# Expert weights of a mixture-of-experts layer in packets of 8 KB instead of 4 KB

## The chip, the core and the metric

The kernel runs on one core of a Trainium2 chip. A core has a matrix engine (PE, with its weight loads shown as PEld), a vector engine (DVE), an activation engine (ACT), GpSimd (POOL) and a queue engine (SP) that here issues nearly all loads from HBM. The transfers themselves are done by 16 DMA engines that work beside the compute engines. The metric is device time in microseconds of one launch; the median of three runs of the kernel before is 1217.87 us (1216.93 to 1220.4).

## What is computed

One layer of a hybrid backbone on 512 tokens of 1024 channels, with 256 context tokens, in fp32. Three token mixers (retention, window attention, neighbourhood attention) are merged by gates and an output projection. Then comes the part that the change is about, an expert-choice SwiGLU mixture of 16 experts, where each expert takes its 64 best tokens:

```python
def expert_choice_ffn(h, w_router, w_gate, w_up, w_down):
    b, n, d = h.shape
    cap = CAPACITY_FACTOR * n // N_EXPERTS                    # 2 * 512 // 16 = 64
    aff = jax.nn.softmax((h @ w_router).astype(jnp.float32), axis=-1)
    gate, idx = lax.top_k(jnp.swapaxes(aff, 1, 2), cap)
    bidx = jnp.arange(b)[:, None, None]
    xe = h[bidx, idx]
    hid = jax.nn.silu(jnp.einsum('becd,edf->becf', xe, w_gate)) * jnp.einsum('becd,edf->becf', xe, w_up)
    ye = jnp.einsum('becf,efd->becd', hid, w_down) * gate[..., None].astype(h.dtype)
    return jnp.zeros_like(h).at[bidx, idx].add(ye)
...
        hx = modulate(rms_norm(x, g_ffn[layer]), mod_x[:, 3], mod_x[:, 4])
        x = x + mod_x[:, 5, None] * expert_choice_ffn(hx, w_router[layer], w_exp_gate[layer],
                                                      w_exp_up[layer], w_exp_down[layer])
    return rms_norm(x, g_final)
```

Each of `w_gate`, `w_up` and `w_down` is 16 matrices of 1024 x 1024 fp32 (4 MB each), 201 MB in all. The rest of the inputs is about 80 MB.

## The kernel before

**Up to the experts.** Until about 640 us the kernel projects, runs the three mixers and merges them. A "pump" (class `Pump`) feeds the projections of `w_in` and of the three output matrices to PE in between: each unit's raw weights are loaded into a buffer of tag `rw` (three of 4 KB a partition), split by ACT (line 294) and DVE (line 295) into a high and a low part in two buffers of tag `ws` (seven of 4 KB), and multiplied three times. The splits run two units ahead of PE, the loads three or more. Beside that, `mod_sums` adds up parts of `w_mod` on DVE (line 1160) from loads of 512 KB (line 1144), one step for every eight steps of the pump. Then the output projection, the router's logits, the selection of tokens and the experts follow.

**The experts' weights** come in 384 chunks of 512 KB, a chunk being 128 neighbouring rows of 1024 floats, one row of 4 KB to a partition. Their order is written out in `chunks` (line 1089 on): for each expert eight chunks of gate and eight of up, alternately, where the first two of each of the next expert stand ahead of this one's eight chunks of the down matrix. `fetch` (line 1103) takes a free buffer off the list `free` and issues the next chunk's load on SP (line 1116); `use` (line 1121) hands the oldest chunk to PE and puts its buffer back on the list. There are 36 buffers: nine of the pool `ring2` from the end of the mixers, four left by `mod_sums`, and 23 that the stages before the experts leave one after the other, of tags `u4` (19 buffers of 4 KB, which hold the normalised input, the mixers' outputs, the merged rows and the residual `acc` earlier), `ws` and `rw`. All loads stand in SP's queue in one order: a load that waits for its buffer holds up those behind it.

**An expert on PE.** `gate_up(e, k)` (line 1513) multiplies the 128 channels of chunk k with the gate and the up matrix, eight matmuls of 512 columns in the records. `hid` is turned by transposes (line 1562), then eight chunks of the down matrix follow (line 1576), and for every second expert the outputs are scattered onto `acc`. For expert 0 the token rows are picked by PE itself (`select`, line 1530) between the steps of `gate_up`; for the others `gather` (line 1453) fetches them by an indirect DMA of POOL. At the end `last_scatter` and `put` finish the last experts, normalise and store.

Of the kernel before, what the change touches and what calls it, by code (L numbers as in the profile page):

```python
# [49 lines left out]
def kernel(ctx, tc, x, c, cctx_x, c_ctx, w_mod, b_mod, g_mix, g_ffn, w_in, decay, ret_gn, w_ret,  # L50
# [8 lines left out]
    RW = 3  # L59
# [15 lines left out]
    U4p = ctx.enter_context(tc.tile_pool(name="u4p", bufs=19))  # L75
# [7 lines left out]
    psp = ctx.enter_context(tc.tile_pool(name="psp", bufs=1, space=bass.MemoryType.PSUM))  # L83

# [117 lines left out]
    hx_ = [[u4([P, 2, S], F32R, name=f"hx{i}{p}") for i in range(4)] for p in "hl"]  # L202
    hc_ = [[u4([P, 4, CTX], F32R, name=f"hc{i}{p}") for i in range(2)] for p in "hl"]

    def HX(k, lo=0):
        return hx_[lo][k // 2][:, k % 2, :]

    def HC(k, lo=0):
        return hc_[lo][k // 4][:, k % 4, :]
# [6 lines left out]
    def row_stat(i0, i1):  # L216
        for i in range(i0, i1):
            junk = ws([P, D], name="junk")
            A.activation(f32(junk), xs[i], AF.Square, accum_out=ssq[:, i:i + 1])
        rsqrt(rstd[:, i0:i1], ssq[:, i0:i1], 1.0 / D, i1 - i0)  # L220
# [60 lines left out]
    class InUnit:  # L281
# [43 lines left out]
    class ProjUnit:  # L325
# [95 lines left out]
    def pair(name):  # L421
        return [u4([P, 2, S], name=name) for _ in range(2)]

    def at(y, k):
        return y[k // 2][:, k % 2, :]

    ropes = {}

    def rope_table(i):
        ropes[i] = u4([P, 2, S], name="rope")  # L430
        SY.dma_start(ropes[i], rope[:, 2 * i:2 * i + 2, :])

    def rope_t(o, i, q):
        cos, sin = ropes[i][:, 0, :], ropes[i][:, 1, :]
# [172 lines left out]
    def proj_unit(br, d, w):  # L607
# [3 lines left out]
        def done(o):  # L611
# [5 lines left out]
            if br == 2:  # L617
                if d % 2 == 0:
                    for p in range(2):
                        mg[p].append(u4([P, 2, S], F32R, name="mg"))  # L620
                hi, lo = mg[0][-1][:, d % 2, :], mg[1][-1][:, d % 2, :]
                A.activation(hi, m_, AF.Copy, scale=0.5)
                V.scalar_tensor_tensor(lo, m_, 0.5, f32(hi), op0=OP.mult, op1=OP.subtract)
# [303 lines left out]
    def window(g):  # L927
# [31 lines left out]
        def value(b, ti):  # L959
# [8 lines left out]
            if ti == len(tiles) - 1:  # L968
                evac(yb[g][:, :, b * P:(b + 1) * P], PVs.pop(b)[:, :256].rearrange("p (i q) -> p i q", i=2))
# [119 lines left out]
    def gate_chunks(e, k0, k1):  # L1089
        for i in range(k0, k1):  # L1090
            for w in (w_g, w_u):
                chunks.append((w, e * D * FH + i * P * FH))

    gate_chunks(0, 0, KT)
    for e in range(NE):
        if e + 1 < NE:
            gate_chunks(e + 1, 0, AHEAD)
        for i in range(KT):
            chunks.append((w_d, e * D * FH + i * P * D))
        if e + 1 < NE:  # L1100
            gate_chunks(e + 1, AHEAD, KT)

    def fetch(most=99):
        while free and len(loaded) < len(chunks) and most:
            most -= 1
            tg = free.pop(0)
            if tg in ("rg", "mw", "mac"):
                t = ring2.tile([P, FH], F32, name="rg", tag=tg, bufs=dict(rg=9, mw=3, mac=2)[tg])
            elif tg == "u":
                t = u4([P, FH], name="rg")  # L1110
            elif tg == "z":
                t = rw([P, FH], "rg")
            else:
                t = wtile([P, FH], "rg")
            w, off = chunks[len(loaded)]
            ld = SY.dma_start(t, dap(w, off, [[FH, P], [1, FH]]))
            if len(loaded) >= PF:
                tc.keep_in_program_order(ld)
# [17 lines left out]
    def mod_sums():  # L1136
        steps = [(w, k) for w in (2, 3, 4, 5) for k in range(KT)]
        tiles = []

        def load():  # L1140
# [6 lines left out]
        load()  # L1147
        load()
        for i, (w, k) in enumerate(steps):
            load()  # L1150
            if k == 0:
                macs[w] = ring2.tile([P, D], F32, name="mac", tag="mac", bufs=2)
# [13 lines left out]
            if k == KT - 1 and w in (3, 4):  # L1166
                o = px()
                for j in range(KT):
                    mm(o[:, 2 * j:2 * j + 2], macs[w][:, j * P:(j + 1) * P], one, True, True)
                dst, b0 = ((sf, 40), (af, 48))[w - 3]  # L1170
                V.tensor_tensor(dst, o[:, 0:2 * KT:2], colv[:, b0:b0 + KT], op=OP.add)
# [23 lines left out]
    R1 = 4  # L1195
# [13 lines left out]
    free.extend(["mw"] * 3 + ["mac"])  # L1209


    accs = []
    for t in range(TT):
        a_ = u4([P, D], name="acc")
        SY.dma_start(a_, dap(x, t * P * D, [[D, P], [1, D]]))
        accs.append(a_)
    free.extend(["u"] * 7)

    def acc(t, sl=slice(0, D)):
        return accs[t][:, sl]  # L1220

    V.scalar_tensor_tensor(af, af, 1.0, colv[:, 56:64], op0=OP.add, op1=OP.mult)
# [4 lines left out]
    SY.dma_start(wr, dap(w_router, 0, [[NE, P], [P * NE, KT], [1, NE]]))  # L1227
# [14 lines left out]
    R2 = 2  # L1242
# [25 lines left out]
    for half in range(2):  # L1268
        o = [pa() for _ in range(TT)]

        def product(t, kx, k0, hi, lo):
            k = k0 + kx
            ts = slice(t * P, (t + 1) * P)
            mh, ml = at(mg[0], k)[:, ts], at(mg[1], k)[:, ts]
# [4 lines left out]
        for k0 in range(0, KT, 2):  # L1279
# [3 lines left out]
            hi, lo = ws([P, 2, 512]), ws([P, 2, 512])  # L1283
# [55 lines left out]
    free.extend(["u"] * 8 + ["w"] * 5 + ["z"] * 2)  # L1339
# [113 lines left out]
    def gather(r):  # L1453
# [59 lines left out]
    def gate_up(e, k):  # L1513
        if k == 0:
            og[e] = [pa(), pa()]
        w = (use(), use())
# [34 lines left out]
    for e in range(NE):  # L1551
# [24 lines left out]
        for f in range(KT):  # L1576
            w = use()
# [18 lines left out]
        for k in range(AHEAD, KT):  # L1596
# [24 lines left out]
    jka = u4([P, 512], name="jka")  # L1621
# [21 lines left out]
    def put(t, helped=()):  # L1643
        ot = u4([P, D], name="ot")
# [99 lines left out]
```

## Time and profile before

| | us |
|---|---|
| median of three runs | 1217.87 |
| the profiled execution, its own time | 1221.08 |
| its span, first to last instruction | 1219.3 |
| PE busy | 1155.5 (95%) |
| DVE busy | 617.3 (51%) |
| ACT busy | 403.9 (33%) |
| mean granted TensorE clock | 0.986 |

All times in the views count from the start of the span. PE's busy time counts matmuls from their start to a modelled end, so a busy PE may still be waiting for data; whether a stage is bound by its loads is read from the DMA rows and from what ended PE's waits.

### The profile page before, as it was taken

What the parts mean: (1) busy time and instruction counts of PE and PEld (TensorE: products, weight loads), DVE (VectorE), ACT (ScalarE), POOL (GpSimd) and SP (SyncE); (2) the same over time, 40 slices, a digit from 0 to 9 for tenths busy, and PEclk for the clock granted to TensorE, in tenths of its full rate; (3) what the DMA queues carried; (4) which work ended last, traced back from release to release, by engine and by line L of the source; (5) the groups of instructions that cost most, each with busy time, mean ns of one, the idle gap of its engine ahead of it and who ended that gap; (6) DMA issues with size and microseconds to landing.
All of it is one profiled execution on the core that took longest, in us unless ns stands there. A gap on an engine that the chain in (4) does not pass through costs nothing.

```text
span 1219.3 us, 15848 instructions
## 1 busy us (share of the span) xinstructions
PE 1155.5 (95%) x5876; PEld 714.0 (59%) x5876; DVE 617.3 (51%) x1380; ACT 403.9 (33%) x779; POOL 87.0 (7%) x150
## 2 busy tenths in 40 slices
PE   4999999999999999999999979999999999999995
PEld 2788888777668887788888744333333323233322
DVE  3687666698867664677646352232332223222213
ACT  4544334576645553232332232112111111111112
POOL 1011211100040220000000000000000000000001
PEclk9999999999999999999999979999999999999998
DMA  9822112111012124887637548999999999999994
GB/s 274 219 87 70 52 52 89 53 36 35 19 52 62 35 61 166 291 268 244 206 103 293 207 173 313 405 409 409 409 409 409 409 409 409 409 409 409 409 409 184
DMA packets 159978, 285.57 MB, mean 234 GB/s; under 512 B 10838, under 2 KB 100250, under 8 KB 159900
## 3 DMA queue, kind: packets, MB, share of 16 engines
q1 hardware_dynamic: 158172, 278.27, 62.6%
q0 software_dynamic: 1152, 4.19, 0.9%
q10 hardware_dynamic: 576, 2.10, 0.4%
q8 instruction: 46, 0.75, 0.3%
q14 instruction: 32, 0.26, 0.1%
HBM read 280.33 MB, written 4.19 MB: 233 GB/s over the span
## 4 chain that ended last, share of the span: by engine, by line
PE 62%; DMA 25%; DVE 7%; ACT 2%; SPq 1%; issue 1%; POOL 1%; DVEq 0%; POOLq 0%; ACTq 0%
PE px L119 26%; DMA rg<-in_w_exp_up_dram 16%; PE pa L67 10%; PE px L67 8%; DMA rg<-in_w_exp_down_dram 8%; PE pa L119 7%; PE PV L119 3%; PE oc L119 3%; PE pa L1041 1%; PE pa L955 1%; DVE ws L295 1%; PE oy L119 1%; DMA wm<-in_w_mod_dram 1%; DVE rt L445 1%; SPq L231 1%
## 5 line engine op out<-in xcount | busy, mean ns | idle before, releaser
L67 PE MATMUL pa<-rg,xe 128*64 128x512 f32 x1024 | 264.5, 609 | 7.3 <-DMA rg<-in_w_exp_up_dram 4.9
L67 PEld LDWEIGHTS pa<-rg,xe 128*64 128x64 f32 x1024 | 72.4, 137 | 155.4 <-issue 108.7
L67 PE MATMUL px<-rg,hid 128*64 128x512 f32 x512 | 120.2, 601 | 10.9 <-DMA rg<-in_w_exp_down_dram 10.2
L295 DVE TENSOR_TENSOR ws<-rw,ws 128x1024 fp32r<-128x1024 f32 x55 | 68.8, 1252 | 55.6 <-PE px L119 34.9
L67 PEld LDWEIGHTS px<-rg,hid 128*64 128x64 f32 x512 | 32.8, 136 | 90.3 <-issue 48.5
L119 PE MATMUL px<-hx0h,ws 128*128 128x512 f32 x224 | 83.3, 401 | 0.0
L119 PE MATMUL px<-hx3h,ws 128*128 128x512 f32 x224 | 83.2, 398 | 0.0
L119 PE MATMUL px<-hx2h,ws 128*128 128x512 f32 x224 | 82.7, 397 | 0.0
L119 PE MATMUL px<-hx1h,ws 128*128 128x512 f32 x224 | 82.6, 398 | 0.0
L67 DVE SCALAR_TENSOR_TENSOR tt<-px,gcol,m 128x512 f32<-128x512 f32 x16 | 12.0, 751 | 127.7 <-PE px L67 127.7
L67 ACT ACTIVATE yy<-tt 64x512 fp32r<-64x512 f32 x32 | 20.1, 628 | 144.6 <-DVE tt L67 144.2
L67 DVE TENSOR_TENSOR acc<-px,acc 128x512 f32<-128x512 f32 x58 | 37.5, 687 | 59.3 <-PE px L67 59.3
L119 PE MATMUL px<-yh,ws 128*128 128x512 f32 x192 | 62.3, 390 | 0.8 <-ACT mod L1165 0.8
L294 ACT ACTIVATE ws<-rw 128x1024 fp32r<-128x1024 f32 x55 | 57.8, 1052 | 6.4 <-DMA rw<-in_w_in_dram 5.9
L911 ACT ACTIVATE Sx<-Sx,nm 128x512 f32<-128x512 f32 (+1 forms) x64 | 47.9, 748 | 34.7 <-DVE nm L947 19.5
L1160 DVE SCALAR_TENSOR_TENSOR mac<-mw,cpad,mac 128x1024 f32<-128x1024 f32 x30 | 38.5, 1283 | 18.9 <-DMA mw<-in_w_mod_dram 16.6
L119 PEld LDWEIGHTS px<-hx3h,ws 128*128 128x128 f32 x224 | 42.1, 189 | 7.9 <-issue 1.1
L119 PEld LDWEIGHTS px<-hx0h,ws 128*128 128x128 f32 x224 | 42.2, 189 | 7.7 <-issue 0.7
L119 PEld LDWEIGHTS px<-hx2h,ws 128*128 128x128 f32 x224 | 42.6, 190 | 7.1 <-issue 0.2
L119 PEld LDWEIGHTS px<-hx1h,ws 128*128 128x128 f32 x224 | 42.2, 188 | 7.2
L67 ACT ACTIVATE gu<-pa 128x512 f32<-128x512 f32 x16 | 9.5, 596 | 110.1 <-PE pa L67 110.1
L67 DVE TENSOR_SCALAR xe<-px,af,sf 128x128 f32<-128x128 f32 (+1 forms) x36 | 14.0, 403 | 61.1 <-ACT xe L67 41.8
(432 smaller groups left out, 2158.2 us busy)
## 6 DMA issues: line engine op xcount, KB each, us to landing
rg<-in_w_exp_gate_dram SPq DMA_DIRECT2D x128, 512.0 KB, 10.2
rg<-in_w_exp_up_dram SPq DMA_DIRECT2D x128, 512.0 KB, 10.2
rg<-in_w_exp_down_dram SPq DMA_DIRECT2D x128, 512.0 KB, 10.2
rw<-in_w_in_dram SPq DMA_DIRECT2D x58, 512.0 KB, 3.8
mw<-in_w_mod_dram SPq DMA_DIRECT2D x32, 512.0 KB, 4.8
wm<-in_w_mod_dram SPq DMA_DIRECT2D x16, 512.0 KB, 7.4
rw<-in_w_out_dram SPq DMA_DIRECT2D x8, 512.0 KB, 3.6
xs<-in_x_dram SPq DMA_DIRECT2D x4, 512.0 KB, 4.2
```

Source lines behind the costliest of these rows:

```text
L67: return (lambda *a_, **k_: tc.keep_in_program_order(f(*a_, **k_))) if pinned[0] else f
L119: PE.matmul(o, lhsT, rhs, start=start, stop=stop)
L231: SY.dma_start(t, dap(w_mod, part * D + k * P, [[NM, P], [P * NM, KT], [1, P]]))
L294: A.activation(hi, raw, AF.Copy)
L295: V.tensor_tensor(lo[:, :NV], raw[:, :NV], f32(hi[:, :NV]), op=OP.subtract)
L445: V.tensor_copy(t2[b:b + q], o[c:c + q])
L911: A.activation(Sx[:, :n], Sx[:, :n], AF.Exp, scale=-1.0, bias=nm, accum_out=l[:, 0:1])
L955: PE.transpose(o[:, j * P:(j + 1) * P], SXs[b, j][:, ti * P:(ti + 1) * P], ident)
L1041: PE.transpose(o[:, b * P:(b + 1) * P], SXs[a, b][:, ti * P:(ti + 1) * P], ident)
L1160: V.scalar_tensor_tensor(macs[w], tiles[i], cpad[:, k, 0:1], macs[w], op0=OP.mult, op1=OP.add)
```

## The change

Two neighbouring rows of an expert's matrix go to one partition, so that one partition's share of a load is 8 KB in one piece; a load is 256 rows, 1 MB, and there are 192 instead of 384. Partition p then holds rows 2p and 2p+1 of the block, and chunk k is every second channel of the block (`ch(d)`). So the operands that meet the chunks are taken with a step of two columns: the tokens that `select` and `gather` turn, the hidden rows before their transposes, the rows for the router and the sums of the modulation; the columns of bias, gain and router weights are brought into the same order once (`colx`, and a second small DMA for `w_router`). The buffers become pairs of 4 KB: `u8` (nine pairs) with a single `u4`, three pairs of `ws`, four single `rw`, and in `ring2` four pairs for the experts, two for `mod_sums` and one for its sums. A pair comes free when both its chunks are used. Eighteen pairs hold weights; one of them ("s") is made of a single `u4` and a single `rw` and is loaded as two DMAs of 4 KB rows, as is the very last block. `fetch(1)` in the pump comes every eighth step instead of every fourth.

```diff
-    RW = 3
+    RW = 4
...
-    U4p = ctx.enter_context(tc.tile_pool(name="u4p", bufs=19))
+    U8p = ctx.enter_context(tc.tile_pool(name="u8p", bufs=9))
+    U4p = ctx.enter_context(tc.tile_pool(name="u4p", bufs=1))
...
+    def ch(d):
+
+        return slice(256 * (d // 2) + d % 2, 256 * (d // 2) + 256, 2)
+
+    def u8(shape, dtype=F32, name="u8"):
+        return U8p.tile(list(shape), dtype, name=name, tag="u8")
...
     def ws(shape, name="ws"):
-        return Wp.tile(list(shape), F32R, name=name, tag="ws", bufs=7)
+        t = Wp.tile([shape[0], 2] + list(shape[1:]), F32R, name=name, tag="ws", bufs=3)
+        return t[:, 0], t[:, 1]
 
     def wtile(shape, name):
-        return Wp.tile(list(shape), F32, name=name, tag="ws", bufs=7)
+        return Wp.tile(list(shape), F32, name=name, tag="rw", bufs=RW)
...
         def split(self, raw):
-            hi, lo = ws([P, KT, P]), ws([P, KT, P])
+            hi, lo = ws([P, KT, P])
...
-    ring2 = ctx.enter_context(tc.tile_pool(name="ring2", bufs=9))
-    PF = 999
-    chunks, loaded, free, used = [], [], ["rg"] * 9, [0]
+    ring2 = ctx.enter_context(tc.tile_pool(name="ring2", bufs=4))
+    BUFS = dict(rg=4, mw=2, mac=1)
+    chunks, loaded, free = [], {}, ["rg"] * 4
     AHEAD = 2
...
-            ld = SY.dma_start(t, dap(w, off, [[FH, P], [1, FH]]))
...
+            if tg == "s" or key == chunks[-1]:
+                t = t if tg == "s" else [t[:, 0, :], t[:, 1, :]]
+                for i in range(2):
+                    SY.dma_start(t[i], dap(w, off + i * FH, [[2 * FH, P], [1, FH]]))
+            else:
+                SY.dma_start(t.rearrange("p i f -> p (i f)"), dap(w, off, [[2 * FH, P], [1, 2 * FH]]))
+                t = [t[:, 0, :], t[:, 1, :]]
+            loaded[key] = (t, tg)
+
+    def use(w, e, k):
+        t, tg = loaded[w, e, k // 2]
+        if k % 2:
+            loaded[w, e, k // 2] = None
+            free.append(tg)
+        return t[k % 2]
...
-                t = ring2.tile([P, D], F32, name="mw", tag="mw", bufs=3)
-                SY.dma_start(t, dap(w_mod, k * P * NM + w * D, [[NM, P], [1, D]]))
-                tiles.append(t)
+                t = ring2.tile([P, 2, D], F32, name="mw", tag="mw", bufs=2)
+                SY.dma_start(t, dap(w_mod, k * P * NM + w * D, [[NM, P], [P * NM, 2], [1, D]]))
+                tiles.extend([t[:, 0, :], t[:, 1, :]])
...
-    R1 = 4
+    R1 = 8
+
+    colx = small([P, 3, KT], "colx")
+    o = px()
+    for h in range(2):
+        for i in range(2):
+            mm(o[64 * h:64 * h + 64, 12 * i:12 * i + 12], ident[:, i:P:2], colv[:, 40 + h:64:2], True, True)
+    V.tensor_copy(colx.rearrange("p q (b i) -> p q b i", i=2), o[:, 0:24].rearrange("p (i q b) -> p q b i", i=2, q=3))
...
-    free.extend(["mw"] * 3 + ["mac"])
+    free.extend(["mw"] * 2)
...
-    free.extend(["u"] * 7)
+    free.extend(["u"] * 3)
...
-    SY.dma_start(wr, dap(w_router, 0, [[NE, P], [P * NE, KT], [1, NE]]))
+    for i in range(2):
+        SY.dma_start(wr[:, i:KT:2, :], dap(w_router, i * NE, [[2 * NE, P], [2 * P * NE, KT // 2], [1, NE]]))
...
-            PE.transpose(o[:, i * P:(i + 1) * P], acc(t)[:, (4 * half + j) * P:(4 * half + j + 1) * P], ident)
+            PE.transpose(o[:, i * P:(i + 1) * P], acc(t, ch(4 * half + j)), ident)
...
-    free.extend(["u"] * 8 + ["w"] * 5 + ["z"] * 2)
+    free.extend(["u"] * 4 + ["w"] * 3 + ["s"])
...
-        w = (use(), use())
+        w = (use("G", e, k), use("U", e, k))
...
-            mm(o[:, :CAP], acc(t)[:, d * P:(d + 1) * P], ohs[:, t, :], t == 0, t == TT - 1)
+            mm(o[:, :CAP], acc(t, ch(d)), ohs[:, t, :], t == 0, t == TT - 1)
...
-                PE.transpose(o[:, j * P:(j + 1) * P], gu[f][:, j * P:(j + 1) * P], ident)
+                PE.transpose(o[:, j * P:(j + 1) * P], gu[f][:, ch(j)], ident)
...
-            w = use()
+            w = use("D", e, f)
```

## Rows read from the trace of the kernel before

**Rows 1.** The page: DMA busy in 40 slices of 30.5 us (tenths), rate, packets by size.

```profile
DMA  9822112111012124887637548999999999999994
GB/s 274 219 87 70 52 52 89 53 36 35 19 52 62 35 61 166 291 268 244 206 103 293 207 173 313 405 409 409 409 409 409 409 409 409 409 409 409 409 409 184
DMA packets 159978, 285.57 MB, mean 234 GB/s; under 512 B 10838, under 2 KB 100250, under 8 KB 159900
```

**Rows 2.** Windows: stretch; length; PE, PEld, DVE, ACT, POOL busy; PEclk, DMA share, GB/s.

```profile
770.00:900.00 130.00, 130.00 (x616) 48.56 (x612) 42.51 (x93) 25.24 (x55) 1.87 (x2) 1.00 1.03 409
900.00:1195.00 295.00, 276.61 (x1128) 91.44 (x1126) 77.33 (x167) 43.95 (x95) 3.75 (x4) 1.00 1.03 409
```

**Rows 3.** Windows, same columns, while rows of w_in and w_mod are loaded.

```profile
42.00:44.00 2.00, 2.00 (x40) 1.59 (x38) 1.02 (x8) 1.05 (x2) 0.00 (x0) 1.00 1.17 293
```

**Rows 4.** The page: the instruction queue (packets, MB); one DMA issue group (KB, us to landing).

```profile
q8 instruction: 46, 0.75, 0.3%
...
rg<-in_w_exp_down_dram SPq DMA_DIRECT2D x128, 512.0 KB, 10.2
```

**Rows 5.** Timeline of SP's issues around the first expert: start, us, line, transfer, count.

```profile
722.24 0.33 SPq L1116 DMA_DIRECT2D rg<-in_w_exp_up_dram  x1
732.63 0.33 SPq L1116 DMA_DIRECT2D rg<-in_w_exp_gate_dram  x1
...
738.37 0.33 SPq L1116 DMA_DIRECT2D rg<-in_w_exp_gate_dram  x1
...
744.17 0.33 SPq L1116 DMA_DIRECT2D rg<-in_w_exp_gate_dram  x1
...
757.49 0.33 SPq L1116 DMA_DIRECT2D rg<-in_w_exp_gate_dram  x1
...
760.38 0.33 SPq L1116 DMA_DIRECT2D rg<-in_w_exp_gate_dram  x1
```

**Rows 6.** Windows, same columns, as the first expert begins.

```profile
725.00:730.00 5.00, 4.68 (x20) 3.94 (x22) 1.90 (x9) 0.40 (x1) 0.00 (x0) 0.50 0.02 10
```

**Rows 7.** Chain of waits, one lap of two experts apart: start, us, what.

```profile
757.47 1.02 PE px L67 x8
...
808.72 1.02 PE px L67 x8
```

**Rows 8.** Timeline of the last expert: start, us, engine, out<-moving,stationary [wait before].

```profile
1178.58 1.93 PE L67 MATMUL pa<-rg,xe 128*64 128x512 f32 x6 [0.22 <-DMA rg<-in_w_exp_up_dram]
...
1179.88 9.25 SPq L1116 DMA_DIRECT2D rg<-in_w_exp_down_dram  x8
...
1180.44 0.66 PE L67 MATMUL px<-cs,oh 128*128 128x128 f32 x4
...
1190.66 1.94 PE L67 MATMUL pa<-rg,xe 128*64 128x512 f32 x8
...
1194.12 7.09 PE L67 MATMUL px<-rg,hid 128*64 128x512 f32 x32
```

**Rows 9.** Timeline of PE: its longest wait for expert weights.

```profile
922.33 1.08 PE L67 MATMUL px<-rg,hid 128*64 128x512 f32 x4 [1.50 <-DMA rg<-in_w_exp_down_dram]
```

**Rows 10.** Windows, same columns, in the routing.

```profile
712.00:714.00 2.00, 0.20 (x2) 0.18 (x2) 1.20 (x6) 0.26 (x1) 0.00 (x0) 0.92 0.24 98
714.00:716.00 2.00, 0.92 (x3) 0.50 (x2) 1.45 (x6) 0.33 (x2) 0.00 (x0) 0.50 1.02 408
```

**Rows 11.** Instruction groups by line: busy, mean ns, idle time before and its releaser.

```profile
L295 DVE TENSOR_TENSOR ws<-rw,ws 128x1024 fp32r<-128x1024 f32 x55 | 68.8, 1252 | 55.6 <-PE px L119 34.9
...
L294 ACT ACTIVATE ws<-rw 128x1024 fp32r<-128x1024 f32 x55 | 57.8, 1052 | 6.4 <-DMA rw<-in_w_in_dram 5.9
...
L1160 DVE SCALAR_TENSOR_TENSOR mac<-mw,cpad,mac 128x1024 f32<-128x1024 f32 x30 | 38.5, 1283 | 18.9 <-DMA mw<-in_w_mod_dram 16.6
```

**Rows 12.** Timeline of PE: products whose stationary operand will be read every second column.

```profile
703.44 0.60 PE L67 MATMUL px<-cs,acc 128*128 128x128 f32 x4
...
738.28 1.10 PE L67 MATMUL px<-ohs,acc 128*128 128x64 f32 x8
```

More of the change, by code (lines that the diff above doesn't have):

```diff
@@ L201 @@
     NM = 6 * D
-    hx_ = [[u4([P, 2, S], F32R, name=f"hx{i}{p}") for i in range(4)] for p in "hl"]
-    hc_ = [[u4([P, 4, CTX], F32R, name=f"hc{i}{p}") for i in range(2)] for p in "hl"]
+    hx_ = [u8([P, 2, 2, S], F32R, name=f"hx{i}") for i in range(4)]
+    hc_ = [u8([P, 2, 4, CTX], F32R, name=f"hc{i}") for i in range(2)]
     def HX(k, lo=0):
-        return hx_[lo][k // 2][:, k % 2, :]
+        return hx_[k // 2][:, lo, k % 2, :]
     def HC(k, lo=0):
-        return hc_[lo][k // 4][:, k % 4, :]
+        return hc_[k // 4][:, lo, k % 4, :]
     ssq = keep.tile([P, 6], F32, name="ssq")
@@ L421, in pair @@
     def pair(name):
-        return [u4([P, 2, S], name=name) for _ in range(2)]
+        return u8([P, 4, S], name=name)
     def at(y, k):
-        return y[k // 2][:, k % 2, :]
-    ropes = {}
+        return y[:, k, :]
+    ropes = []
     def rope_table(i):
-        ropes[i] = u4([P, 2, S], name="rope")
-        SY.dma_start(ropes[i], rope[:, 2 * i:2 * i + 2, :])
+        if not ropes:
+            ropes.append(u8([P, 4, S], name="rope"))
+        SY.dma_start(ropes[0][:, 2 * i:2 * i + 2, :], rope[:, 2 * i:2 * i + 2, :])
     def rope_t(o, i, q):
-        cos, sin = ropes[i][:, 0, :], ropes[i][:, 1, :]
+        cos, sin = ropes[0][:, 2 * i, :], ropes[0][:, 2 * i + 1, :]
         t1, t2 = h2(name="rt1"), h2(name="rt2")
@@ L618, in done @@
                 if d % 2 == 0:
-                    for p in range(2):
-                        mg[p].append(u4([P, 2, S], F32R, name="mg"))
-                hi, lo = mg[0][-1][:, d % 2, :], mg[1][-1][:, d % 2, :]
+                    mg.append(u8([P, 2, 2, S], F32R, name="mg"))
+                hi, lo = mg[-1][:, 0, d % 2, :], mg[-1][:, 1, d % 2, :]
                 A.activation(hi, m_, AF.Copy, scale=0.5)
@@ L1083, with gate_chunks @@
     ph1.close()
-    ring2 = ctx.enter_context(tc.tile_pool(name="ring2", bufs=9))
-    PF = 999
-    chunks, loaded, free, used = [], [], ["rg"] * 9, [0]
+    ring2 = ctx.enter_context(tc.tile_pool(name="ring2", bufs=4))
+    BUFS = dict(rg=4, mw=2, mac=1)
+    chunks, loaded, free = [], {}, ["rg"] * 4
     AHEAD = 2
[L1089 to L1094, printed above, removed]
+    W = dict(G=w_g, U=w_u, D=w_d)
+    def gate_chunks(e, b0, b1):
+        for b in range(b0, b1):
+            chunks.extend([("G", e, b), ("U", e, b)])
+    gate_chunks(0, 0, KT // 2)
     for e in range(NE):
         if e + 1 < NE:
-            gate_chunks(e + 1, 0, AHEAD)
-        for i in range(KT):
-            chunks.append((w_d, e * D * FH + i * P * D))
+            gate_chunks(e + 1, 0, AHEAD // 2)
+        chunks.extend(("D", e, b) for b in range(KT // 2))
         if e + 1 < NE:
-            gate_chunks(e + 1, AHEAD, KT)
+            gate_chunks(e + 1, AHEAD // 2, KT // 2)
     def fetch(most=99):
@@ L1138, in mod_sums @@
         tiles = []
+        mac = ring2.tile([P, 2, D], F32, name="mac", tag="mac", bufs=1)
         def load():
@@ L1168, in mod_sums @@
                 for j in range(KT):
-                    mm(o[:, 2 * j:2 * j + 2], macs[w][:, j * P:(j + 1) * P], one, True, True)
-                dst, b0 = ((sf, 40), (af, 48))[w - 3]
-                V.tensor_tensor(dst, o[:, 0:2 * KT:2], colv[:, b0:b0 + KT], op=OP.add)
+                    mm(o[:, 2 * j:2 * j + 2], macs[w][:, ch(j)], one, True, True)
+                V.tensor_tensor((sf, af)[w - 3], o[:, 0:2 * KT:2], colx[:, w - 3, :], op=OP.add)
             yield
@@ L1208, with acc @@
         pass
-    free.extend(["mw"] * 3 + ["mac"])
-    accs = []
+    free.extend(["mw"] * 2)
+    accs = [u8([P, 2, D], name="acc") for _ in range(2)]
+    def acc(t, sl=slice(0, D)):
+        return accs[t // 2][:, t % 2, sl]
     for t in range(TT):
-        a_ = u4([P, D], name="acc")
-        SY.dma_start(a_, dap(x, t * P * D, [[D, P], [1, D]]))
-        accs.append(a_)
-    free.extend(["u"] * 7)
-    def acc(t, sl=slice(0, D)):
-        return accs[t][:, sl]
-    V.scalar_tensor_tensor(af, af, 1.0, colv[:, 56:64], op0=OP.add, op1=OP.mult)
+        SY.dma_start(acc(t), dap(x, t * P * D, [[D, P], [1, D]]))
+    free.extend(["u"] * 3)
+    V.scalar_tensor_tensor(af, af, 1.0, colx[:, 2, :], op0=OP.add, op1=OP.mult)
     sf2 = sf[:, :, None].to_broadcast([P, KT, 2])
@@ L1241 @@
     lg_o = []
-    R2 = 2
+    R2 = 1
     ss2 = small([P, 2, TT], "ss2")
@@ L1620 @@
     ss3, rs3 = small([P, 2, TT], "ss3"), small([P, TT], "rs3")
-    jka = u4([P, 512], name="jka")
+    ots = [u8([P, 2, D], name="ot") for _ in range(2)]
     def last_scatter(t):
```

66 lines of the change are left out of this document (30 added, 36 removed).

## The prediction

> **What bounds the kernel now.** The page's slices come first: in which part do the DMA engines never rest? In two: the first slice, and from about 760 us to the end. In between DMA has room in nearly every slice [rows 1]. The windows settle the second part: 409 GB/s without a break from 770 to 1195 us, while PE still has 130 of 130 us busy up to 900, and 277 of 295 after it [rows 2]. So the rate is set by the transfers, at first behind a stock of loaded chunks, then with PE waiting for each. The lap of PE over two experts, while stock lasts, is 808.7 - 757.5 = 51.2 us, 25.6 for an expert [rows 7]; 24 chunks at 409 GB/s need 24 x 524288 B / 409 = 30.8. PE has 17% to spare, so a faster transfer moves the end. Two places are not bound by it: the start, where all 36 buffers are full, DMA rests (0.02 busy) and each load waits for PE to give a buffer back [rows 5, 6], and the last 41 us, where PE runs on what has landed [rows 8].
>
> **The rate.** What does a packet of 8 KB cost? The trace has none from SP's queue, so it is bounded by the sizes it has. At 409 GB/s over 16 engines a 4 KB packet takes 16 x 4096 / 409 = 160.2 ns [rows 2]; the 512 B pieces of w_in and w_mod, with engines as full, go at 293 GB/s, 28.0 ns each [rows 3]. A line through both has (160.2 - 28.0) / 3584 = 0.0369 ns per byte and 9.1 ns per packet. On it an 8 KB packet takes 311.3 ns, 155.6 for each 4 KB: 421 GB/s. A chunk of 512 KB is eight packets to an engine, so it takes 1.282 us now and 1.245 then, 0.0364 less. Ends: nothing gained, if the 9.1 ns are not per packet; and twice as much, 0.0728, if all of it went, which no finite packet gives. I take the line, between two sizes that run on the same queue.
>
> **What it is worth.** Only loads that are issued into a busy queue gain. Now the 36th buffer is loading at 722.2, the next loads come at 732.6, 738.4 and so on, two for every step of 2.9 us (2.56 us of transfer), and from 760.4 they come faster than they can be served, with 54 chunks done [rows 5]. The loads then set the time until PE gets gate and up of step 3 of the last expert, chunk 368, at 1178.6 [rows 8]: 314 chunks x 0.0364 = **11.4 us saved**. One pair in 18 keeps 4 KB rows: **+0.6**.
>
> **Later start.** A pair returns only after the second step. So the first refill comes at 738.4 instead of 732.6, then four chunks every 5.8 us (4.98 us of transfer), at 744.2, 750.0, and at 755.6, one step ahead of 757.5. From there the queue stays full: the next four come at 760.4 and 755.6 + 4.98 = 760.6. It has 36 + 12 = 48 chunks done then, and reaches 54 at 755.6 + 6 x 1.245 = 763.1, where the old one stood at 760.4: **+2.7 us** (ends: 0, if the queue catches up as it has pauses to give, and 5.7, all of the first delay).
>
> **Tail.** Now step 2 is multiplied while step 3 lands. With pairs both wait for the same load, and the eight matmuls of one step, 1.94 us, move behind it [rows 8]. From there PE has work: step 4 and 5 land 4.98 us later, and steps 2 and 3 with the turned one-hots take 2 x 1.94 + 0.66 and a product of acc. The last down chunks, 16 x 1.245 = 19.9 us behind, are wanted from 17.5 to 24 us behind. **+1.9 us**, ends 0 and 3.7.
>
> **Order of channels.** Four small products and a copy make colx: four at the 0.14 us of the nearest row (eight in 1.10 us) [rows 12], on a PE that is full then: **+0.5**, ends 0 and 1. The products with every second column read the same number of values; the trace has none with such a step, so I take 0, and the end above is a rival below. A second DMA for w_router lies in the early queue and is wanted 600 us later: 0.
>
> **Buffers in pairs, before the experts.** At 0 each, with the cover: (a) A split now waits for a whole pair. ACT's half takes 1.05 us and DVE's 1.25 [rows 11]; DVE waits for PE already (55.6 us over 55 splits, about 1 us each), and ACT would now wait as long and hold up the softmax and copies queued behind it. PE wants the result two units later, a unit being at least 4.7 us of matmuls. Without that cover it would be 55 x 1.05 = 58 us, so I keep +2 for some of them. (b) w_mod comes in 16 loads of two steps instead of 32; DVE has waited 18.9 us for them [rows 11], with lo parts and merges queued behind. A load is still issued two steps, that is 16 steps of the pump, ahead: 0, end +1. (c) SP's queue now holds 1 MB where it held 512 KB, ahead of w_in and w_out; with one more raw buffer these stand one unit earlier: 0, ends -1 and +1. (d) SP issues as one of its loads lands, and 10.2 us to landing are eight loads of 1.28 us in flight [rows 4]; eight of 1 MB hide more, so no gap comes from there. The indirect gather shares the engines with longer packets and lands later, which PE's spare 17% takes.
>
> **Sum:** -11.4 + 0.6 + 2.7 + 1.9 + 0.5 = -5.7 us. The profiled execution took 1221.1 us, its span 1219.3: it would be 1215.4, with a span of 1213.6. The median shown is 3.2 us below that execution; the same gain takes 1217.9 to **1212.2 us**.
>
> **The rivals.** (1) The change doesn't do what it says: the queue cuts 8 KB into 4 KB packets, or those cost twice as much. For it: of 159978 packets only 78 are of 8 KB or more [rows 1], 46 of them loads of instructions of 16 KB [rows 4]. Against: these show that larger packets exist. Then nothing is saved and the terms of pairs stay: 2.9 + 1.9 + 0.5 = 5.3, **1223.2 us**. The Trainium skill, DMA: Bandwidth & Descriptors, section SWDGE vs HWDGE vs iDMA, speaks against the change here: a packet of the software path is best kept to 4096 B. No row shows whether SP's path cuts; by that rule it would be this rival.
> (2) The short pieces lose for another reason, such as their scattered rows, and only a third of the 9.1 ns is per packet: 314 x 0.0121 = 3.8 saved, 5.3 lost, **1219.4**. For it: the line has only two points, and the short one reads 512 B out of long rows. The Trainium skill, DMA: Bandwidth & Descriptors, section Why small descriptors are slow, puts the loss at about 3 cycles for a packet of beats of 32 B; its rate for 512 B would be (16/19) / (128/131) = 0.86 of that for 4 KB, where the rows have 293 / 409 = 0.72, so the trace does not agree.
> (3) Slower, by one mechanism: a weight load of every second column takes r times as long. It lies on PE's path where no stock covers it: eight groups of transposes of acc of 0.6 us, two selects at half clock (16 products of twice 0.14 us), six of 1.1 us, and the last expert's two groups of 0.66 us [rows 8, 12]: 4.8 + 4.5 + 6.6 + 1.3 = 17 us in all. The cost is 17 x (r - 1), so it eats the gain from r = 1.34; at r = 2 it gives 1212.2 + 17 = **1229 us**. Against: the same values are read, and in the experts' later stage it is hidden. The Trainium skill, SBUF — State Buffer, Door 1, says fp32 may step up to four elements before its 16-byte lines cost; no run here shows it.
> (4) PE's clock. With pairs PE waits for an up load after its gate load, most of the 2.49 us that 1 MB takes, at a stretch, where the longest wait for weights was 1.5 [rows 9]. In the routing the granted clock fell from full to 0.50 (1.2 GHz) after a stretch with PE busy 0.2 of 2 us [rows 10]. A fall before the last steps costs up to 3.7 us more in the tail. If it falls at every expert, PE becomes the bound once 30.6 / 25.6 - 1 = 19% of its work runs at half clock (an expert's loads then take 24 x 1.247 + 0.6); with a third it is 34.1 us for an expert, 13 x 3.5 = 45 us, **1258 us**. Against: between 900 and 1195 us the clock stayed at 1.00 with 295 - 277 = 18 us of waits [rows 2].
>
> **How the numbers follow.** About 0.3%, 3.7 us, is what a measurement can tell here from no change. The forecast has 0.70; its own range goes from 1206 (late start 0, split and raw buffers better) to 1218 (5.7 for the start, 3.7 for the tail). Rival 1 has 0.12, rival 2 0.06, rival 3 0.05, the tail alone of rival 4 0.04 and its bound 0.03. Of the forecast 0.07 ends within 0.3%. Faster: 0.63 + 0.02 of the tail; same: 0.07 + 0.06 + 0.02 + 0.02 of small r + 0.02 of rival 1 with a small gain; slower: 0.10 + 0.03 + 0.03. The range for 8 in 10 reaches from 1205 to 1221 and leaves out most of rivals 1, 3 and the bound of 4.
>
> **What would show it.** The windows from 800 us on at 419 to 422 GB/s, and packets of 8 KB on SP's queue (about 137000 packets in all instead of 160000); SP's first refill near 738 instead of 732.6; at the end both steps 2 and 3 behind one wait. Wrong if the rate stays at 409, if eight products of acc with a step of two take longer than 1.10 us, if the windows after 900 us show a clock below 1, or if PE shows new waits before 640 us.

## The result and the profile after

The changed kernel takes 1208.5 us (median of six runs, 1206.1 to 1212.3; a second series of six gave 1208.6), the kernel before 1217.7 beside it: 0.9917 of the time, 95% interval 0.9900 to 0.9933, a gain of **9.2 us** where 5.7 were forecast. The profiled execution of the changed kernel took 1206.1 us, its span 1204.3.

The page first: DMA busy by slices, rate, packets by size.

```profile
DMA  9922122110021215897636467999999999999994
GB/s 273 276 73 70 37 66 76 53 36 19 19 71 36 62 62 200 266 285 236 202 91 258 161 259 264 412 420 420 420 420 419 420 422 420 419 422 419 421 420 160
DMA packets 133669, 285.52 MB, mean 237 GB/s; under 512 B 7702, under 2 KB 97114, under 8 KB 110428
```

The same bytes as in [rows 1] go in 26300 packets fewer, and 23241 packets now have 8 KB or more. (The forecast of 137000 left out 3136 packets under 512 B that went too.) The windows that answer to [rows 2]:

```profile
770.00:900.00 130.00, 130.00 (x602) 49.35 (x598) 42.05 (x90) 23.48 (x50) 1.87 (x2) 1.00 1.01 420
900.00:1175.00 275.00, 255.62 (x1081) 96.63 (x1079) 73.30 (x160) 42.56 (x92) 3.75 (x4) 0.98 1.01 420
```

420 GB/s without a pause where 409 stood, one below the forecast of 421. The second window also shows something new: a granted clock of 0.98 instead of 1.00. SP's issues around the first expert, for [rows 5]:

```profile
717.04 0.33 SPq L1133 DMA_DIRECT2D rg<-in_w_exp_up_dram  x1
730.36 0.33 SPq L1133 DMA_DIRECT2D rg<-in_w_exp_gate_dram  x1
...
736.26 0.33 SPq L1133 DMA_DIRECT2D rg<-in_w_exp_gate_dram  x1
...
742.17 7.05 SPq L1133 DMA_DIRECT2D rg<-in_w_exp_down_dram  x4
752.89 0.33 SPq L1133 DMA_DIRECT2D rg<-in_w_exp_gate_dram  x1
```

The first refill stands 10.2 us behind the first product of the selection (720.14), where it was 7.3 us behind it (725.32). A pair comes back one step later, as forecast; that step is 2.9 us here, and not the 5.8 us of 738.4 - 732.6, because PE was at full clock again sooner (granted clock 0.69 in the first 10 us of the selection, 0.50 before). From there two pairs come every 5.9 us, as forecast. PE from expert 14 to the last down loop, for [rows 8]:

```profile
1132.38 3.60 PE L67 MATMUL pa<-rg,xe 128*64 128x512 f32 x6 [1.41 <-DMA rg<-in_w_exp_up_dram]
...
1154.98 7.04 PE L67 MATMUL px<-rg,hid 128*64 128x512 f32 x32
1161.84 4.06 PE L67 MATMUL pa<-rg,xe 128*64 128x512 f32 x16
1165.84 0.66 PE L67 MATMUL px<-cs,oh 128*128 128x128 f32 x4
...
1179.59 7.09 PE L67 MATMUL px<-rg,hid 128*64 128x512 f32 x32
```

Steps 2 and 3 of the last expert stand in one block of 16 products behind one load; the 4.06 us, where 16 take 3.65 elsewhere, hold a wait of 0.4, so the pair landed at about 1162.2. The last down loop starts 17.4 us later; before it was 1194.12 - 1178.58 = 15.5.

Three cuts divide the span: the first product of the selection, the landing of the last gate and up pair, and the end. Before: 725.3, then 453.3, then 40.7 us. After: 720.1, then 442.1, then 42.1. So the two profiled executions differ by -5.2, -11.1 and +1.4 us. The first of these was forecast as 0, and the experiments had to say what of it belongs to the change.

### The profile page after: what moved, and what is told of

The parts are those of the page before. It is cut to its first block, busy times and chain, and to the rows that moved or that the text cites. A ratio compares the mean times of both kernels' runs of the same rounds, so it can differ in the third digit from the quotient of the medians.

```text
span 1204.3 us, 15433 instructions
## 1 busy us (share of the span) xinstructions
PE 1140.5 (95%) x5884; PEld 724.2 (60%) x5884; DVE 614.4 (51%) x1381; ACT 403.9 (34%) x779; POOL 87.2 (7%) x150
## 4 chain that ended last, share of the span: by engine, by line
PE 67%; DMA 22%; DVE 6%; ACT 2%; SPq 1%; POOL 1%; issue 1%; DVEq 0%; POOLq 0%; ACTq 0%
PE px L128 29%; PE pa L67 11%; DMA rg<-in_w_exp_up_dram 10%; PE px L67 9%; PE pa L128 7%; DMA rg<-in_w_exp_gate_dram 6%; DMA rg<-in_w_exp_down_dram 5%; PE PV L128 3%; PE oc L128 3%; PE pa L966 1%; PE pa L1052 1%; PE oy L128 1%; DMA wm<-in_w_mod_dram 1%; DVE rt L455 1%; SPq L240 0%
## 5 line engine op out<-in xcount | busy, mean ns | idle before, releaser
L128 PE MATMUL px<-hx,ws 128*128 128x512 f32 x1344 | 367.6, 398 | 0.0
L67 PE MATMUL pa<-rg,xe 128*64 128x512 f32 x1024 | 259.1, 613 | 19.4 <-DMA rg<-in_w_exp_up_dram 16.2
L128 PEld LDWEIGHTS px<-hx,ws 128*128 128x128 f32 x1344 | 243.3, 189 | 42.9 <-issue 3.1
L67 PE MATMUL px<-rg,hid 128*64 128x512 f32 x512 | 113.3, 595 | 0.1
L128 PE MATMUL oc<-hc,ws 128*128 128x256 f32 x384 | 85.5, 283 | 0.0
L128 PEld LDWEIGHTS oc<-hc,ws 128*128 128x128 f32 x384 | 69.6, 189 | 9.4 <-DVE vt L525 0.3
L922 ACT ACTIVATE Sx<-Sx,nm 128x512 f32<-128x512 f32 (+1 forms) x64 | 47.8, 747 | 30.9 <-DVE nm L958 15.5
L137 DVE TENSOR_TENSOR ws<-rw,ws 128x512 fp32r<-128x512 f32 (+1 forms) x32 | 26.3, 822 | 37.7 <-ACT ws L136 37.6
L128 PEld LDWEIGHTS px<-yh,ws 128*128 128x128 f32 x192 | 36.1, 188 | 7.7 <-ACT ws L303 0.2
L128 PE MATMUL pa<-ws,mg 128*128 128x512 f32 x168 | 39.8, 394 | 0.0
L67 ACT ACTIVATE xe<-px,sf,af 128x128 f32<-128x128 f32 (+1 forms) x36 | 15.4, 449 | 66.1 <-PE px L67 58.4
```

The source lines that it names most:

```text
L67: return (lambda *a_, **k_: tc.keep_in_program_order(f(*a_, **k_))) if pinned[0] else f
L128: PE.matmul(o, lhsT, rhs, start=start, stop=stop)
L137: V.tensor_tensor(lo, src, f32(hi), op=OP.subtract)
L922: A.activation(Sx[:, :n], Sx[:, :n], AF.Exp, scale=-1.0, bias=nm, accum_out=l[:, 0:1])
```

## The experiments

**The packets alone.** Every pair of the changed kernel is loaded as two rows of 4 KB; order, pairs and strides stay.

```diff
-            if tg == "s" or key == chunks[-1]:
+            if True:
```

> The changed kernel with one thing undone: each pair is loaded by two DMAs of 4 KB rows instead of one of 8 KB rows. Pairs, order of channels and buffers stay. If the packet size makes the gain, the rate falls from 420 to 409 GB/s and the time rises by what the prediction gave the packets, 10.8 us, from 1208.5 to about 1219. If the gain comes from the buffers and the order before the experts, it stays at 1208 to 1210. By the prediction's own terms for pairs (5.3 us on the kernel before) it would be 1223; what it lies below that is a gain that the prediction did not have.

It took 1219.6 us, 1.0006 of the time before (0.9994 to 1.0018). Windows from 770 and 900 us on, and the last pair:

```profile
770.00:900.00 130.00, 128.30 (x596) 48.70 (x596) 40.22 (x89) 25.24 (x54) 1.88 (x2) 1.00 1.03 409
900.00:1170.00 270.00, 245.30 (x1041) 88.67 (x1042) 73.79 (x159) 39.58 (x87) 3.75 (x4) 0.99 1.03 409
```

```profile
1177.40 3.65 PE L67 MATMUL pa<-rg,xe 128*64 128x512 f32 x14 [1.48 <-DMA rg<-in_w_exp_up_dram]
```

Back to 409 GB/s, and the gain is gone. The packets are worth 1219.6 - 1208.5 = 11.1 us, and the stretch from the selection to the last pair says the same (453.2 against 442.1 us); all else in the change costs 1.6 us by the medians, 0.7 by the ratio, which the noise does not tell from nothing.

**Smaller pieces.** Each pair in two loads whose pieces are 2 KB.

```diff
-                SY.dma_start(t.rearrange("p i f -> p (i f)"), dap(w, off, [[2 * FH, P], [1, 2 * FH]]))
+                for j in range(2):
+                    SY.dma_start(t[:, :, 512 * j:512 * j + 512], dap(w, off + 512 * j, [[2 * FH, P], [FH, 2], [1, 512]]))
```

> The changed kernel with each pair loaded by two DMAs of 2 KB pieces (half the columns of both rows). If each packet costs 9.1 ns beside its bytes, a 2 KB packet takes 84.7 ns, the rate is 387 GB/s, a chunk takes 1.355 us, 0.110 more than with 8 KB, and the time is 1208.5 + 314 x 0.110 x 17/18 = about 1241 us. If only a third of the 9.1 ns is per packet, the chunk loses 0.024 us against 4 KB and the time is about 1227.

1242.2 us (ratio 1.0187, 1.0161 to 1.0213) at 388 GB/s: the 1241 of the line, and not the 1227 that rival 2 gives.

**The loads by themselves.** A kernel of stages, each loading the same volume in one size of piece, with all computation left out.

```diff
+                tc.keep_in_program_order(SY.dma_start(t[:, :width], dap(w, off, [[step, P], [1, n]])))
```

> Loads alone, on SP's queue, in packets of one size after the other: 512 B, 1, 2, 4, 8 and 16 KB, each piece followed by a gap of its own length, then 4, 8 and 16 KB without gaps; all computation is left out. A line of 0.0369 ns per byte and 9.1 ns per packet gives 293, 349, 387, 409, 421 and 427 GB/s. If the queue cuts at 4 KB, 8 and 16 KB run at 409. If the short pieces lose by their scattered rows, 512 B to 2 KB lie below the line through 4 and 8 KB, and the pieces with gaps below those without.

One window of each stage: 512 B, 1, 2, 4, 8 and 16 KB cut out of longer rows, then 4 and 8 KB without gaps. The columns are DVE, POOL, clock, share, GB/s.

```profile
20.00:30.00 10.00, 0.00 (x0) 0.00 (x0) 1.00 1.19 290
80.00:90.00 10.00, 0.00 (x0) 0.00 (x0) 1.00 1.10 348
120.00:130.00 10.00, 0.00 (x0) 0.00 (x0) 1.00 1.05 387
170.00:180.00 10.00, 0.00 (x0) 0.00 (x0) 1.00 1.03 410
200.00:210.00 10.00, 0.00 (x0) 0.00 (x0) 1.00 1.01 420
250.00:260.00 10.00, 0.00 (x0) 0.00 (x0) 1.00 1.01 429
290.00:300.00 10.00, 0.00 (x0) 0.00 (x0) 1.00 1.02 408
320.00:330.00 10.00, 0.00 (x0) 0.00 (x0) 1.00 1.02 424
```

The line through two sizes of the kernel before gave 293, 349, 387, 409, 421 and 427; all six lie within about 1%. At 4 and 8 KB gaps between the pieces change no more than that (8 KB without gaps has 422 from 340 to 350 us, 16 KB 428 from 360 to 390). The loss of short pieces thus goes with their number; pieces below 4 KB without gaps were not run. Nor is it the number of loads: 4 KB had 16 loads of 1 MB with gaps and 32 of 512 KB without.

**One raw buffer more and one split buffer fewer, in the kernel before.**

```diff
-    RW = 3
+    RW = 4
...
-        return Wp.tile(list(shape), F32R, name=name, tag="ws", bufs=7)
+        return Wp.tile(list(shape), F32R, name=name, tag="ws", bufs=6)
```

> The kernel before with one part of the change alone: four raw buffers instead of three and six buffers for split weights instead of seven (the number of chunk buffers stays 36). The first select starts 5.2 us earlier in the profile of the changed kernel, where the prediction had 0. If the raw buffer makes that, this gives 1217.7 - 5 = about 1213 us and a first select near 720 us. If the prediction's 0 is right for this part, 1217 to 1219 and a first select near 725.

1219.3 us, ratio 1.0000 (0.9984 to 1.0017), selection at 726.0: the two together give nothing.

**The changed kernel again, unedited.**

> The changed kernel once more, unedited, as the anchor for the three beside it. Its first profiled execution began the first product of the token selection at 720.1 us, the kernel before at 725.3, and two edits of the one or the other at 724.2 and 726.0. If the earlier selection belongs to the change, it stands at 720 here too; if it is the scatter of one execution, it stands nearer to 724, and the time is 1208.5 as the median was.

1208.6 us, selection at 722.3. Five executions of kernels with 8 KB packets show it at 720.1, 722.3, 722.4, 722.6 and 723.5, four of kernels with single buffers or one kind of pairs at 724.9 to 726.0. The two kernels with the same buffers and smaller packets, above, have 724.2 and 724.1. So about 3 us of the first cut belong to the change, and 2 us of the 5.2 to the one execution (its first 40 us were already 2.4 us shorter).

Counted from the first product that turns yn, near 108 us, this scatter is gone: to the selection it is 617.3 us in the kernel before and 614.1 to 614.4 in the five with 8 KB packets. The two with smaller packets have 615.9. There PE ran at half clock longer near 240 us; the kernel with 4 KB rows, then the changed one:

```profile
240.00:242.00 2.00, 2.00 (x8) 1.69 (x7) 1.57 (x3) 0.31 (x1) 0.82 (x1) 0.50 0.35 92
```

```profile
240.00:242.00 2.00, 2.00 (x11) 1.69 (x11) 1.89 (x5) 0.08 (x1) 1.05 (x1) 0.99 0.45 129
```

**One pair of buffers fewer.**

```diff
-    BUFS = dict(rg=4, mw=2, mac=1)
-    chunks, loaded, free = [], {}, ["rg"] * 4
+    BUFS = dict(rg=3, mw=2, mac=1)
+    chunks, loaded, free = [], {}, ["rg"] * 3
```

> The changed kernel with one pair of buffers fewer for expert weights (17 pairs instead of 18; three instead of four in the ring made after the mixers). Theory that the stock at the start counts: before the first expert the DMA engines rest with every buffer full, so a pair less is one load of 2.49 us that has to be made later, while the loads set the time: 1211.0 us, with the last gate and up pair landing 2.5 us later in the span. Rival, that the pauses of the first expert give the queue room to catch up (the case in which the prediction's +2.7 for the later start becomes 0): the refills begin 5.8 us earlier in PE's order and the time stays at 1208.5.

1210.7 us, 2.1 more, in intervals that overlap (0.9919 to 0.9957 against 0.9904 to 0.9937). The profile is clearer: from the selection (722.56) to the last pair 445.3 us, where it was 442.2.

```profile
1167.83 3.65 PE L67 MATMUL pa<-rg,xe 128*64 128x512 f32 x14 [1.35 <-DMA rg<-in_w_exp_up_dram]
```

The 3.1 us are one load (2.49) or a little more: the queue doesn't catch up.

**No step of two columns.**

```diff
-        return slice(256 * (d // 2) + d % 2, 256 * (d // 2) + 256, 2)
+        return slice(128 * d, 128 * d + 128)
```

> The changed kernel with every operand of a step of two columns read as 128 neighbouring columns instead, in all transposes, the selection, the gather and the modulation sums; the loads keep their packets of 8 KB, so the channels no longer meet their weights and the output is not the layer's. It prices the step of two by itself. By the prediction's rival 3, with the ratio of 1.48 that the weight loads of the transposes show (208 ns against 141), 17 us x 0.48 = 8.2 us would be saved: 1200.3 us. By the prediction's 0: 1208.5. By the pitch of the products, which rose from 1.09 to 1.22 us for eight transposes and not at all for the selection, only the eight groups of four and two groups of eight on the bound path count, 0.03 and 0.13 us each: 0.5 us, 1208.0.

The channels then no longer meet their weights, so only the time counts. 1206.8 us, 1.8 less, again with overlapping intervals (0.9885 to 0.9920). The 8.2 us of rival 3 are excluded; between 0 and 3 us the times don't decide. The profiles speak for the low end: from the selection to the last pair 442.4 us where the changed kernel has 442.2, from there to the end 41.9 where it has 42.0. The weight loads of the changed kernel, then of the kernel before (groups by line: busy, mean ns):

```profile
L67 PEld LDWEIGHTS px<-cs,gu 128*128 128x128 f32 x128 | 16.6, 208 | 13.3 <-issue 11.4 <-ACT gu L67 1.6 <-DVE gu L67 0.3
```

```profile
L67 PEld LDWEIGHTS px<-cs,gu 128*128 128x128 f32 x128 | 13.7, 141 | 13.4 <-issue 11.4 <-ACT gu L67 1.6 <-DVE gu L67 0.4
```

and products of the changed kernel that answer to [rows 12]:

```profile
698.40 0.63 PE L67 MATMUL px<-cs,acc 128*128 128x128 f32 x4
...
730.26 1.16 PE L67 MATMUL px<-ohs,acc 128*128 128x64 f32 x8
```

The load of a transpose takes 1.48 times as long, but most of that lies beside the product before it: four transposes take 0.63 us instead of 0.60, eight products of the selection 1.16 instead of 1.10 (the expectation, which had them unchanged, read them at half clock), eight transposes 1.22 instead of 1.09.

**Carries before the last pair.**

```diff
-    EARLY = {3: (0, 0, pa), 4: (0, 1, pa), 5: (3, 0, OC), 6: (1, 0, px)}
+    EARLY = {6: (1, 0, px)}
+    SOON = {1: (0, 0, pa), 3: (0, 1, pa), 5: (3, 0, OC)}
...
+            if e == NE - 2 and f in SOON:
+                carry(*SOON[f])
```

> The changed kernel with three of the four products that carry acc into the last sums moved from behind the last gate and up pair into the down loop of the expert before it. They are 3 x 1.06 = 3.2 us of PE's 17.4 us between that pair and the last down loop. If PE has room in the down loop, waiting for its loads, the end comes 3.2 us earlier: 1205.3 us. If PE and the loads meet there (in the profile the down loop ends at 1161.84 and the pair lands at 1162.26, with PE busy 40 of 40 us around it), the products only move the wait: at most 0.4 us, 1208.1.

1209.5 us (0.9905 to 0.9944): no gain. PE around the last pair:

```profile
1166.32 1.94 PE L67 MATMUL px<-rg,hid 128*64 128x512 f32 x8
1168.08 3.60 PE L67 MATMUL pa<-rg,xe 128*64 128x512 f32 x16
...
1182.96 7.09 PE L67 MATMUL px<-rg,hid 128*64 128x512 f32 x32
```

The wait is gone, but PE arrives later: from the selection to the last pair 444.6 us where 442.2 stood, and from there to the end 39.5 where 42.0 stood. PE had waited at most 1.05 us for that pair (in the second profile of the changed kernel), so the loops before it have no room for the 3.2 us that were moved.

**What made the selection earlier.** Two parts of the buffers in pairs, each alone in the kernel before, then both. The split buffers:

```diff
-        return Wp.tile(list(shape), F32R, name=name, tag="ws", bufs=7)
+        t = Wp.tile([shape[0], 2] + list(shape[1:]), F32R, name=name, tag="ws", bufs=3)
+        return t[:, 0], t[:, 1]
```

> The kernel before with only the split buffers in pairs (three pairs of ws instead of seven singles, four rw instead of three; a split waits for a whole pair), everything else with 4 KB packets and single chunks as before. In the profiled executions the first product of the token selection began at 725.3 and 726.0 us with single split buffers and at 722.3 to 723.5 in four executions of the changed kernel's family (720.1 in one where the first 60 us were shorter). Theory: it is the pairs of split buffers that shorten the stages before the experts, since ACT and DVE then take the splits in another rhythm and the waits of PE for DVE between 240 and 650 us (2.6 us in the kernel before, none in the changed one) go: selection at about 722.5, time 1217.9 - 3 = 1215 us. Rival: it comes from the loads of the modulation sums or from elsewhere: selection at 725 to 726, 1218 us.

1217.3 us (0.9977 to 1.0008), selection at 725.2. The loads of w_mod:

```diff
-                t = ring2.tile([P, D], F32, name="mw", tag="mw", bufs=3)
-                SY.dma_start(t, dap(w_mod, k * P * NM + w * D, [[NM, P], [1, D]]))
+                t = ring2.tile([P, 2, D], F32, name="mw", tag="mw", bufs=2)
+                SY.dma_start(t, dap(w_mod, k * P * NM + w * D, [[NM, P], [P * NM, 2], [1, D]]))
```

> The kernel before with only the loads of w_mod for the modulation sums in pairs (16 loads of 1 MB into two pairs of buffers instead of 32 of 512 KB into three single ones), the expert weights with 4 KB packets as before. DVE waited 18.9 us for these loads in the kernel before and 7.6 us in the changed one. Theory that this shortens the stages before the experts: selection at about 722.5 us, time 1215 us. Rival, that DVE's waits for w_mod are hidden and the pairs of split buffers do it, or nothing that can be named: selection at 725 to 726, 1218 us.

1217.5 us (0.9979 to 1.0004), selection at 724.9. Alone, each interval holds 1, and neither makes the 3 us. Both together:

> The kernel before with both edits of e9_split_pairs and e10_mod_pairs: the split buffers and the loads of w_mod in pairs, the expert weights in single chunks with 4 KB packets as before. Alone the first gave a selection at 725.24 us and the second one at 724.85, where the kernel before had 725.32. Theory that each part brings a little and that they add up or help each other: selection near 722.5 us and a time of 1215 us. Rival, that neither makes the earlier selection of the changed kernel: selection at 724.5 or later, 1217 us or more.

1214.4 us, ratio 0.9964 (0.9950 to 0.9978): 3.8 us by the medians, 2.7 to 6.1 by the interval. Counted from yn, the selection comes after 616.8 us with the split buffers, 616.6 with w_mod, and 614.9 with both, although there PE ran at half clock as long near 240 us as with 4 KB rows (0.50 from 240 to 242). The selection and the last pair with both:

```profile
723.06 3.67 PE L67 MATMUL px<-ohs,acc 128*128 128x64 f32 x16 [0.99 <-DVE ohs L67]
```

```profile
1173.42 1.93 PE L67 MATMUL pa<-rg,xe 128*64 128x512 f32 x6 [0.21 <-DMA rg<-in_w_exp_up_dram]
```

PE's waits between 240 and 660 us seem to say why neither is enough (who waits for whom: us in total, times, longest). The kernel before:

```profile
PE pa L580 <- DVE nm L1031: 1.2, 1, 1.2
PE px L119 <- ACT mod L1165: 0.8, 1, 0.8
PE pa L119 <- DVE qs L453: 0.4, 1, 0.4
PE PV L119 <- DVE PT L925: 0.2, 1, 0.2
```

With the split buffers in pairs:

```profile
PE px L120 <- DVE gt L615: 1.0, 1, 1.0
```

With the loads of w_mod in pairs:

```profile
PE pa L580 <- DVE nm L1031: 1.3, 1, 1.3
PE pa L119 <- DVE qs L453: 0.3, 1, 0.3
PE PV L119 <- DVE PT L925: 0.2, 1, 0.2
```

The first takes away the waits in the mixers, but PE then waits for DVE in the merge; the second takes away the one in the merge. With both, as in the changed kernel, this view has no wait: 2.6 us are gone. But before 240 us waits have grown; the kernel before, then both parts:

```profile
PE pa L883 <- DVE yn L877: 3.6, 4, 3.0
```

```profile
PE pa L884 <- DVE yn L878: 5.7, 4, 4.2
PE pa L869 <- ACT yt L865: 0.8, 1, 0.8
```

That is 2.9 us more. So over the whole stretch from 40 to 660 us PE rests as long as before: 7.5 us in the kernel before, 8.0 with both parts, 7.6 in the changed kernel (620 less the first number behind the length):

```profile
40.00:660.00 620.00, 612.50 (x3389) 489.00 (x3388) 431.21 (x951) 283.34 (x516) 64.55 (x104) 1.00 0.36 111
40.00:660.00 620.00, 611.97 (x3395) 491.25 (x3395) 430.37 (x953) 282.97 (x516) 64.65 (x104) 0.99 0.36 114
40.00:660.00 620.00, 612.38 (x3400) 491.88 (x3390) 427.13 (x947) 284.28 (x517) 64.57 (x104) 1.00 0.37 115
```

PE's waits have moved, and their sum has not fallen; so they are not shown to be the cause. The kernel with one raw buffer more says the same: 0.5 us of waits after 240 us, 6.1 for yn before it, and no earlier selection. What the traces show is that PE's products themselves take less time in places: from the first product with vn to the first with yh, where PE is busy throughout, 138.5 us with the split buffers in pairs, alone or with both, against 141.1 in the kernel before and 141.0 with w_mod alone. The order of PE's products differs there; why it is quicker stays open.

## Why the prediction was right, point by point

The forecast of 1212.2 us lies 3.7 above the measured 1208.5, and the step on the early buffers makes up that difference.

**The rate was right.** 11.4 - 0.6 = 10.8 us forecast, 11.1 measured. The line from two sizes of the kernel before held from 512 B to 16 KB. Rival 1 fell: the queue moves packets of 8 KB and more as they are. The software path's 4096 B, which the Trainium skill (DMA: Bandwidth & Descriptors, section SWDGE vs HWDGE vs iDMA) prefers, is no limit on SP's path here: 23241 packets had 8 KB or more, at 420 GB/s. Rival 2 fell with the 388 GB/s of 2 KB pieces. By an estimate from the loss of about 3 cycles for a packet, which the Trainium skill (DMA: Bandwidth & Descriptors, section Why small descriptors are slow) states, 512 B would run at 0.86 of the rate of 4 KB; the loads alone show 290 / 410 = 0.71.

**Pairs of chunks.** The kernel with both parts of the early pairs (1214.4) and the one with 4 KB rows (1219.6) differ by what the pairs of chunks, the order of channels and the strides cost: 5.2 us, where start, tail and colx were forecast at 2.7 + 1.9 + 0.5 = 5.1. The two intervals leave it about 2 us of play, so that it came out this close is in part luck. The profiles of the two divide it:

| term | forecast | measured | from |
|---|---|---|---|
| later start | +2.7 | +2.9 | selection to last pair, 453.2 against 450.4 us |
| tail | +1.9 | +1.7 | last pair to the end, 42.1 against 40.4 us |
| colx, strides | +0.5 | within the rest | 5.2 less both; strides 0 to 3 by their own run |

The profiled execution of the kernel before had 453.3 us in the middle stretch, four other executions with single chunks 450.4, 450.4, 450.4 and 451.3. Its granted clock was 0.50 and 0.89 in the first and second 10 us of that stretch, that of the kernel with one raw buffer more 0.60 and 1.00, so PE got through the first expert later and gave its buffers back later. Against this execution alone the start would seem to cost nothing. The stock run, and the four others, say that the queue does not catch up.

**Early buffers: the step that failed.** Forecast 0 with ends that added up to -1 and +4; measured -3.8. The raw buffer is 0, as forecast. The splits and w_mod were called covered, and in the sum they cost nothing: ACT waits for PE now, as the step said. Groups for [rows 11]:

```profile
L304 DVE TENSOR_TENSOR ws<-rw,ws 128x1024 fp32r<-128x1024 f32 x55 | 67.3, 1225 | 17.0 <-ACT ws L303 16.8
...
L303 ACT ACTIVATE ws<-rw 128x1024 fp32r<-128x1024 f32 x55 | 57.9, 1054 | 24.8 <-PE px L128 16.3 <-issue 8.3
...
L1177 DVE SCALAR_TENSOR_TENSOR mac<-mw,cpad,mac 128x1024 f32<-128x1024 f32 x30 | 38.5, 1282 | 7.6 <-DMA mw<-in_w_mod_dram 7.1
```

But the step asked only whether a longer wait on ACT or DVE would reach PE. Some did: the new waits of PE before 640 us, a sign of being wrong by the prediction, are there (in the changed kernel 5.5 us for yn instead of 3.6, and 0.8 for yt). It didn't ask what another order of the engines could save. DVE's waits for w_mod fell from 18.9 to 7.6 us, those of the splits from 55.6 to 17.0, PE's waits after 240 us went, and some of its products took less time. That both parts together make -3.8 us is measured; which of these makes it stays open. The measured terms, -3.8 + 5.2 - 11.1, make -9.7 where the medians have -9.2 (they are differences of the same runs, so this is no check of its own); without the early one they make -5.9 against the forecast's -5.7.

**Rivals 3 and 4.** Rival 3 exists in small: products of acc took 1.16 us where the text said above 1.10 would be wrong, r = 1.05, and 17 x 0.05 = 0.9 us. Rival 4's waits came: mostly 1.3 to 1.7 us for the up load behind the gate load (1.94 once in the second profile). So did the fall of the clock below 1, another sign of being wrong, but not as a bound:

```profile
940.00:960.00 20.00, 18.04 (x67) 5.72 (x64) 4.70 (x7) 3.03 (x5) 0.00 (x0) 0.91 1.01 420
1010.00:1020.00 10.00, 10.00 (x36) 3.39 (x34) 1.90 (x4) 1.78 (x3) 0.00 (x0) 0.85 1.01 422
1130.00:1140.00 10.00, 8.59 (x28) 2.59 (x30) 2.39 (x5) 3.04 (x5) 0.00 (x0) 0.83 1.02 421
```

Some experts lose one or two us at half clock and PE's spare time takes it; the transfers stay at 420 to 422 GB/s throughout, and the last stretch, with 17.4 us to the down loop, is at full clock. Pairs of chunks aren't needed for a fall: the kernel with both early parts and single chunks has 0.83 from 980 to 990 us.

## What to carry to other kernels

Two packet sizes that the trace already holds, with engines full in both, give a line per packet and per byte that prices a third size; here it was right to 1%. A change of granularity is paid at the two ends, where loads do not set the pace: in the stock's first refill and in the last load; price both from the order of the steps, and take the stretch between two cuts from several executions before believing a term of 2 us. Where buffers change in the stages that PE sets, ask what a new order can save as well as what it can cost, and list PE's waits over the whole of those stages: in part of them they went away here, and their sum stayed.

## What the runs showed of the hardware

A load on SP's queue pays about 9 ns for each packet by the line through 290, 348, 387, 410, 420 and 429 GB/s from 512 B to 16 KB; at 4 and 8 KB it is within 1% the same whether the pieces lie side by side or apart (408 and 424 GB/s). A weight load of every second fp32 column took 208 ns in transposes instead of 141, of which little reached PE's pace (eight transposes 1.22 us instead of 1.09). The granted clock fell beside PE's waits: in 900 to 1175 us it was 0.98, with stretches of 10 us down to 0.83 beside waits of 1.3 to 1.5 us, where the kernel before had 1.00 [rows 2] with a longest wait of 1.50 [rows 9]. What in the waits makes the difference these runs don't show.
